# A copy between two places in memory: 8 KB packets cut into 4 KB packets

## The chip, the cores and the metric

The kernel runs on one core of a Trainium2 chip. The core has five engines with instruction queues of their own (TensorE, VectorE, ScalarE called ACT, GpSimd called POOL, and SyncE called SP) and 16 DMA engines that move data. The metric is the device time of one execution in microseconds (us). The time before is the median of three runs, 821.59 us, with runs from 820.93 to 823.31. Lower is better.

## The reference

```python
x = np.random.randn(8192, 8192).astype(np.float32)
return np.fft.ifftshift(x)
```

For even sizes this swaps the quadrants: output row r, column c is input row (r + 4096) mod 8192, column (c + 4096) mod 8192. Nothing is computed, every number only changes its place. The matrix has 8192 x 8192 x 4 bytes = 268.44 MB, and each byte is read once and written once, both in the chip's memory (HBM).

## The kernel before, in words

A row has 32 KB, and each half of it, left or right, is 16 KB that come in one piece from a half row of the input. So the unit of the kernel is the half row.

The kernel consists of DMA copies alone, straight from the input to the output in memory; no tile is loaded into the core. The inner function `copy(queue, row, col, dims)` (line 29 on) makes one copy: it works out the source from the row and column of the output, and issues at line 31 with the access pattern `dims`. Its argument `max_dma_last_dim=piece * 4` bounds the bytes of one contiguous run. `piece` is `hc // 2` = 2048 numbers, so a half row of 4096 numbers (`hc`) becomes two runs of 8192 bytes, and each run is one packet for a DMA engine.

A big copy takes 256 half rows (`rows` = 16 x 16), 4 MB in 512 packets, spread over the 16 DMA engines with 32 packets each, and one more small packet per engine that raises the copy's semaphore when its data has landed. Two queues issue:

- SP issues the left halves (`nc.sync`), 32 copies of 256 half rows.
- ACT issues the right halves (`nc.scalar`), 31 copies of 256 half rows and one of 240. The 16 rows that the last one leaves out go first, in seven small copies of column strips (`strip` = 1024 numbers, runs of 4096 bytes).

The big loop goes through the matrix from the bottom up, in steps of 1024 rows; in each step SP takes the four groups of 256 rows in the order 3, 2, 1, 0, and ACT takes them in the order 1, 0, 3, 2, so that the two queues are two groups apart.

No copy depends on another one's data. The framework gives each copy one of eight semaphores in turn. A copy that gets a semaphore again waits for the copy which had it before, and so each queue has at most four big copies under way at a time. Apart from that, an issuing instruction ends when its packets have found room in the DMA engines' queues. The program ends when SP has seen all eight semaphores at their last value.

Of the kernel before, what the change touches and what calls it, by code (L numbers as in the profile page):

```python
# [1 line left out]

# [4 lines left out]


ENGINES = 16


@with_exitstack
def kernel(
    ctx: ExitStack,
    tc: tile.TileContext,
    x: bass.AP,
    out: bass.AP,
):


    nc = tc.nc
    R, C = x.shape
    hr = R // 2
    hc = C // 2
    per = 16
    rows = ENGINES * per
    piece = hc // 2

    def copy(queue, row, col, dims):
        src = (row + hr) % R * C + (col + hc) % C  # L30
        queue.dma_start(
            out=bass.AP(out.tensor, out.offset + row * C + col, dims),
            in_=bass.AP(x.tensor, x.offset + src, dims),
            max_dma_last_dim=piece * 4,
        )

    start = R - 3 * rows
    strip = hc // 4
    for n, k in enumerate((14, 9, 4)):
        col = hc + n * strip  # L40
        copy(nc.scalar, start + rows - ENGINES, col, [[C, k], [1, strip]])
        copy(nc.scalar, start + rows - ENGINES + k, col, [[C, ENGINES - k], [1, strip]])
    copy(nc.scalar, start + rows - ENGINES, hc + 3 * strip, [[C, ENGINES], [1, strip]])

    for first in range(R - 4 * rows, -1, -4 * rows):
        for n in (3, 2, 1, 0):
            copy(nc.sync, first + n * rows, 0, [[C, rows], [1, hc]])
            right = first + (n + 2) % 4 * rows
            left_out = ENGINES if right == start else 0
            copy(nc.scalar, right, hc, [[C, rows - left_out], [1, hc]])  # L50


# [1 line left out]
_INS = ['x']  # L54
_OUTS = [((8192, 8192), 'float32')]


# [23 lines left out]
```

## Time and profile before

| what | value |
|---|---|
| median of 3 runs | 821.59 us (820.93 to 823.31) |
| the profiled execution | 823.05 us |
| its span, first to last instruction | 821.3 us |
| DMA engines' mean rate | 327 GB/s copied |
| packets | 33888, 268.44 MB |
| share of the span on queue q1 (SP) and q10 (ACT) | 50.6% and 48.4% |
| a big copy, from issue to landing | 102 us |

The profile's page has a strip with a digit for each fortieth of the span, in which 9 stands for DMA engines that are busy for 90% or more, and under it the rate in GB/s. The share of a queue is the time that its packets took, divided by 16 engines times the span. A rate counts each byte once, although it is read and written. The instructions of SP and ACT are listed with the time from their start to their end, which is the time of issuing and not that of moving data. Every copy has the line of `queue.dma_start`, L31, so queues and sizes tell them apart and not lines.

The trace holds a record of each single packet as well: its queue, size, start and duration. It doesn't hold which of the 16 engines ran it.

### The profile page before, as it was taken

To read this page: it belongs to the slowest core of one execution; us is meant where nothing else is said; L and a number is where in the kernel's file an instruction comes from. 1 tells how busy PE (TensorE), PEld (TensorE's weight loads), DVE (VectorE), ACT (ScalarE), POOL (GpSimd) and SP (SyncE) were. 2 spreads that over 40 slices of the span, in tenths; PEclk is the share of its full clock that TensorE was granted. 3 is DMA by queue.
4 is the path that set the end of the run, shared out by engine and by line. 5 is a ranking of instruction groups with operands and counts; after the bars stand their busy time and mean duration, and the time that the engine had idled before them with its cause. 6 is when DMAs were issued, how large, how long until landed. Compare 5 with 4: busy or idle time off the path is not lost. (4 is left out here: it accounts for less than half of the span.)

```text
span 821.3 us, 116 instructions
## 1 busy us (share of the span) xinstructions
POOL 0.2 (0%) x4
## 2 busy tenths in 40 slices
POOL 0000000000000000000000000000000000000000
DMA  9999999999999999999999999999999999999998
GB/s 294 321 328 338 324 329 333 329 331 331 332 329 333 328 330 332 327 328 329 327 334 322 328 322 334 331 327 330 323 331 333 325 332 330 320 330 328 335 326 281
DMA packets 33888, 268.44 MB, mean 327 GB/s; under 512 B 1088, under 2 KB 1088, under 8 KB 1152
## 3 DMA queue, kind: packets, MB, share of 16 engines
q1 hardware_dynamic: 16896, 134.22, 50.6%
q10 hardware_dynamic: 16992, 134.22, 48.4%
HBM read 268.44 MB, written 268.44 MB: 654 GB/s over the span
## 5 line engine op out<-in xcount | busy, mean ns | idle before, releaser
L65 POOL MEMSET const-bfloat16-1.0<- 128x1 bf16 x1 | 0.1, 102 | 0.0
L65 POOL MEMSET const-uint8-127<- 128x1 uint8 x1 | 0.1, 101 | 0.0
L65 POOL MEMSET const-float32-0.0<- 128x1 f32 x1 | 0.1, 99 | 0.2 <-issue 0.2
L65 POOL MEMSET const-float32-1.0<- 128x1 f32 x1 | 0.1, 98 | 0.0
## 6 DMA issues: line engine op xcount, KB each, us to landing
out_dram<-in_x_dram SPq DMA_DIRECT2D x32, 4096.0 KB, 102.0
out_dram<-in_x_dram ACTq DMA_DIRECT2D x31, 4096.0 KB, 102.1
out_dram<-in_x_dram ACTq DMA_DIRECT2D x1, 3840.0 KB, 30.2
out_dram<-in_x_dram ACTq DMA_DIRECT2D x1, 64.0 KB
out_dram<-in_x_dram ACTq DMA_DIRECT2D x1, 56.0 KB
out_dram<-in_x_dram ACTq DMA_DIRECT2D x1, 48.0 KB
out_dram<-in_x_dram ACTq DMA_DIRECT2D x1, 36.0 KB
out_dram<-in_x_dram ACTq DMA_DIRECT2D x1, 28.0 KB
```

What stands on the lines that cost most here:

```text
L65: nc = _bacc.Bacc("TRN2", target_bir_lowering=False, num_devices=1)
```

## The change

`piece` becomes a quarter of a half row instead of a half of it. A half row is then moved as four packets of 4096 bytes one behind the other instead of two of 8192 bytes.

```diff
     per = 16
     rows = ENGINES * per
-    piece = hc // 2
+    piece = hc // 4
 
     def copy(queue, row, col, dims):
         src = (row + hr) % R * C + (col + hc) % C
```

The copies, their order, their queues, their rows and their semaphores stay. The shape of a big copy as the instruction carries it goes from 256x2x2048 to 256x4x1024 numbers, that of the copy of 240 half rows from 240x2x2048 to 240x4x1024. The seven strips have runs of 4096 bytes already and stay as they are.

## The prediction

> **What bounds the kernel now.** I read the page's engine rows first, then the DMA rows, then the queues by stretch, then the issuing instructions.
>
> ```profile
> span 821.3 us, 116 instructions
> ...
> POOL 0.2 (0%) x4
> ...
> DMA  9999999999999999999999999999999999999998
> GB/s 294 321 328 338 324 329 333 329 331 331 332 329 333 328 330 332 327 328 329 327 334 322 328 322 334 331 327 330 323 331 333 325 332 330 320 330 328 335 326 281
> DMA packets 33888, 268.44 MB, mean 327 GB/s; under 512 B 1088, under 2 KB 1088, under 8 KB 1152
> ...
> q1 hardware_dynamic: 16896, 134.22, 50.6%
> q10 hardware_dynamic: 16992, 134.22, 48.4%
> HBM read 268.44 MB, written 268.44 MB: 654 GB/s over the span
> ```
>
> No engine computes; the 16 DMA engines are busy in every slice and the rate is flat. The chain of waits ends after 0.4 us and is of no use here: the end is set by packets alone. Queue q1 carries SP's copies, q10 ACT's. Of the 33888 packets, 1088 are semaphore writes under 512 B, 64 are the 4 KB packets of the seven strips, and the other 32736 are of 8 KB, 2046 for each of 16 engines.
>
> The packets' time: (50.6% + 48.4%) x 16 x 821.3 us = 13010 us. Less 1088 semaphore writes at 9 ns (10 us) and 64 strip packets at 193 ns (12 us), that is 12988 / 32736 = 397 ns for one 8 KB packet. Per engine 2046 x 397 ns = 812 us; the first packet starts at 2.2 us, the last ends at 820.1 us, and the rest is skew between engines and the closing semaphores. The span is therefore packet time, and the question is only what two packets of 4 KB cost against one of 8 KB.
>
> The trace's record of single packets divides the 397 ns: 19535 of the 32736 take 307 to 310 ns, the shortest there are, and the other 13201 take 527 ns in the mean, up to 1476. So an undisturbed 8 KB packet costs 309 ns (424 GB/s over 16 engines), and a mean of 88 ns is stall, spread unevenly: some packets wait long, most not at all.
>
> The strips are the one place where 4 KB packets run, beside 8 KB packets of the other queue. The queue rows of the stretch 5 to 12.4 us, then a stretch's table:
>
> ```profile
> DMA packets 388, 2.53 MB, mean 342 GB/s; under 512 B 50, under 2 KB 50, under 8 KB 108
> ...
> q1 hardware_dynamic: 280, 2.29, 92.5%
> q10 hardware_dynamic: 108, 0.24, 10.1%
> ```
>
> ```profile
> 5.00:12.40 7.40, 0.00 (x0) 1.00 1.03 342
> ...
> 100.00:300.00 200.00, 0.00 (x0) 1.00 1.00 331
> ...
> 804.00:815.00 11.00, 0.00 (x0) 1.00 1.00 333
> ```
>
> Here q1's 280 packets are all of 8 KB, and 0.925 x 16 x 7.4 us / 280 = 391 ns each. Of q10's 108, 50 are semaphore writes and 58 of 4 KB, which take 196 ns in the single record (the rounded share gives 198). Two make 391 ns too: in this stretch a pair costs what one 8 KB packet costs. But it is no ordinary stretch: from 6 to 15 us under a tenth of q1's packets are near 309 ns, where the run has 60%; nearly all are held back a little. In the table the last column is GB/s: one queue alone at the end (333) moves no less than two together (331), so taking turns between queues is not what stalls.
>
> Last come the issuing instructions: those that write the output, SP's waits, and a row of the DMA issues.
>
> ```profile
> L31 ACTq DMA_DIRECT2D out_dram<-in_x_dram x39: 567/20750/27276, 0.7 to 732.1; - x39
> L31 SPq DMA_DIRECT2D out_dram<-in_x_dram x32: 572/18603/22165, 0.7 to 700.7; - x32
> ...
> SPq L31 <- DMA out_dram<-in_x_dram: 240.6, 29, 25.2
> ...
> out_dram<-in_x_dram SPq DMA_DIRECT2D x32, 4096.0 KB, 102.0
> ```
>
> In the first two lines, min, median and max in ns: an issue takes 0.57 us where its queue has room, and some 20 us where it has to wait for room. SP also waits 240.6 us for older copies. Landing 102 us after issue at one copy each 25.5 us per queue means four copies deep.
>
> **The change, part by part.**
>
> *Twice the packets.* Bytes, rows, row order, copies and semaphores stay; 32736 packets become 65472, so 2046 more per engine, all on the path. Their price: the shortest 4 KB packet takes 159 ns, so an undisturbed pair takes 318 against 309, 9 ns more. Ends: if all 9 ns show and the stalls stay, 2046 x 9 = +18.4 us; if stalls shrink by as much, nothing. Below nothing too: all 64 strip packets average 193 ns, a pair 386, which is 11 ns under the run's 397: -22 us. Above: the strip packets that start from 6 to 9 us average 214 ns, a pair 428 against 396 for q1's packets there: +32 ns, +65 us if it held throughout. Between these ends I go by the two rows that compare sizes under one load: packets that are held back anyhow pay nothing (391 against 391), packets at the engine's own pace pay 9 ns (318 against 309), and 60% of the run's packets are of the second kind: 0.6 x 9 = 5.4 ns, 2046 x 5.4 = +11.0 us.
>
> The Trainium skill ("DMA: Bandwidth & Descriptors", section "Why small descriptors are slow") puts the fixed cost at about 3 cycles per packet; at its 850 MHz that is an estimated 3.5 ns, or +7.2 us here in place of the 18.4 us that the shortest packets give, for a median of 829 us. The trace's 9 ns is larger, and the measurement decides; both have the same sign.
>
> *Issue.* All 64 big copies carry twice the packets. A 16-packet strip took 567 ns to issue and a 512-packet copy 572 ns, so packet count costs the issuer nothing while the queue has room. If it doubled, 0.6 us per copy would lie beside the three copies still queued (some 75 us of work): nothing on the path, except about 0.6 us at the very start if that cover is missing.
>
> *Depth.* At the end of a 20.75 us issue about 27 of 33 packets per engine have drained since it began, so 4 x 33 - 27 = 105 packets wait in each engine's queue (an estimate). If that number is the queue's limit, then in 4 KB packets it is 420 KB instead of 840 KB, some 42 us of work per queue. The 16 completions of one copy spread over only 1 to 4 us, so no engine runs dry: nothing. What is late next is the issuer: an issue grows to about 26 us, back to back, and SP's 240.6 us of waits mostly vanish. Nothing else is behind them on SP or ACT. If the queue held under 10 packets this cover would be gone.
>
> *Ends.* The 2.2 us before the first packet and the last microseconds stay.
>
> Sum: the profiled execution took 823.05 us (span 821.3, 1.75 us around it), 1.46 us above the median of 821.59. 823.05 + 11.0 - 1.46 = 832.6, say 833 us.
>
> **The rivals.**
>
> *Memory sets the pace (nothing).* For it: the pair's 391 ns; 327 GB/s in each direction, 654 in all, flat for 800 us, with one queue or two; the engines' own 309 ns would allow 424, and 318 still 412. A slower engine would then merely stall less: 2046 x 0 = 821.6 us. Against it: 60% of packets run at the full 309 ns, so memory is not short at each moment; the packets that start from 12.4 to 35 us move 316 GB/s and those after them 334, so the rate goes with which rows meet, as with conflicts and not a fixed cap. The Trainium skill ("HBM Reference", section "Specifications (TRN2)") gives about 716 GB/s to a domain; 654 is 91% of it, near enough that this rival keeps a chance, not so near as to decide.
>
> *Shorter packets break up the stalls (the other side).* The 527 ns packets hold an engine and the rows it reads and writes; with 4 KB an engine turns to its other queue's rows twice as often, and a blocked stream holds up half as much. It wins once stall falls by over 9 of 88 ns per 8 KB, a tenth. For it: the pair of 386 ns over all strips. Against it: one queue alone, with no other to turn to, is no slower. At 386 ns, 821.6 - 22 = 799 us; at half that gain, 810 us.
>
> *Memory works worse on 4 KB.* Twice as many jumps between streams cause more conflicts, and stall grows. For it: the 428 ns above, and the mean of q1's packets (407 ns from 100 to 700 us) against q10's (386), which shows that row position alone moves 5%. Against it: those are 15 packets. At a third of that price 843 us, at all of it 887.
>
> *The split doesn't happen.* The issued shape changes from 256x2x2048 to 256x4x1024 elements on all 64 copies, so this has next to no chance.
>
> **How the numbers follow.** Less than 0.3% (2.5 us) can't be told from no change here. Part of 9 ns shows, 824 to 840 us: 0.42, predicted 833. Memory paces, 819 to 824: 0.13. Stalls break up, 798 to 819: 0.30. Memory works worse, 840 to 887: 0.15. Faster 0.30, same 0.13, slower 0.57. Cases of both signs count, so the range reaches from 806 (leaving out about a third of the faster case, 0.10) to 850 (leaving out 0.08); the forecast's own range is 824 to 840.
>
> **What would show it.** Queue rows with 66,600 packets, 65,500 of them 4 KB, at 99% share: the split and that packets still set the end. Single packets with a shortest time of 159 ns and a mean near 201 ns ((397 + 5) / 2): the price. A mean of 198 ns says memory paces, 193 that stalls break up, above 206 that memory works worse. ACT and SP issues near 26 us and SP's waits near zero, with landing down to about (105 + 65) x 0.4 = 68 us: the depth. Any stretch with a DMA share under 0.9 would say that queues run dry, and that the depth step is wrong. What would undo the forecast most easily is the stall: at 88 ns of 397 it is ten times the term that I price.

## The result, and the profile after

The changed kernel takes 829.42 us (median of 4 runs, 828.25 to 831.32) against 822.45 us (4 runs, 820.93 to 823.71, three of them those that I had when I predicted). The medians differ by 7.0 us; the ratio is 1.0076, 95% interval 1.0054 to 1.0099, which is 6.3 us (4.4 to 8.1). The forecast was 833 us, 806 to 850. The same kernel was timed again on another chip, where the kernel before is a little faster too: 814.28 us (6 runs) against 811.71 us (20 runs), ratio 1.0041 (1.0027 to 1.0054), which is 3.3 us (2.2 to 4.4). So the sign is firm, and the size differs between the two. From here on they are called the first comparison and the repeat, with their sizes by the ratio.

The profiled execution after took 829.02 us, its span 827.2 us. First the lines of its page that answer to those of before:

```profile
span 827.2 us, 116 instructions
...
DMA  9999999999999999999999999999999999999998
GB/s 293 315 335 329 317 338 327 331 329 324 330 329 329 325 330 324 321 338 326 329 320 325 333 324 322 326 331 326 328 326 318 329 328 324 329 317 323 333 324 274
DMA packets 66624, 268.44 MB, mean 325 GB/s; under 512 B 1088, under 2 KB 1088, under 8 KB 66624
...
q1 hardware_dynamic: 33280, 134.22, 50.1%
q10 hardware_dynamic: 33344, 134.22, 49.6%
```

The packets have doubled, the 1088 semaphore writes have not, and the DMA engines are as full as before. The rate is lower by 2 to 3 GB/s in each of the stretches below, with no gap anywhere. First two stretches of the run before (the last column is GB/s, the one before it the DMA share; it moved 331 from 100 to 300 us and 333 from 804 to 815), then those of the run after:

```profile
300.00:500.00 200.00, 0.00 (x0) 1.00 1.00 329
500.00:700.00 200.00, 0.00 (x0) 1.00 1.00 329
```

```profile
100.00:300.00 200.00, 0.00 (x0) 1.00 1.01 328
300.00:500.00 200.00, 0.00 (x0) 1.00 1.00 327
500.00:700.00 200.00, 0.00 (x0) 1.00 1.00 326
804.00:815.00 11.00, 0.00 (x0) 1.00 1.00 331
```

Then the issuing instructions (min, median and max in ns), SP's waits and a row of the DMA issues, all of the run after:

```profile
L31 ACTq DMA_DIRECT2D out_dram<-in_x_dram x39: 570/25311/28012, 0.7 to 763.3; - x39
L31 SPq DMA_DIRECT2D out_dram<-in_x_dram x32: 654/25169/47445, 0.7 to 724.5; - x32
...
SPq L31 <- DMA out_dram<-in_x_dram: 11.6, 2, 6.6
...
out_dram<-in_x_dram SPq DMA_DIRECT2D x32, 4096.0 KB, 82.1
```

An issue now takes 25 us, one behind the other, and SP's waits for older copies fell from 240.6 to 11.6 us: the issuers wait for room in place of a semaphore. It costs nothing, since the engines never run dry.

One number in these lines does not fit the others. The shares give (50.1% + 49.6%) x 827.2 = 824.7 us of packets per engine, before 99.0% x 821.3 = 813.1: 11.6 us more. But the span grew by only 5.9 us. The records of single packets say what the shares say: a 4 KB packet takes 201.1 ns in the mean (shortest common duration 159), so a pair takes 402.2 against 396.7 ns, and 5.5 ns x 2046 = 11.3 us. Records have grown by twice what the clock shows. The experiments explain that first.

### The profile page after: what moved, and what is told of

The parts are those of the page before. It is cut to its first block, busy times and chain, and to the rows that moved or that the text cites. A ratio compares the mean times of both kernels' runs of the same rounds, so it can differ in the third digit from the quotient of the medians.

```text
span 827.2 us, 116 instructions
## 1 busy us (share of the span) xinstructions
POOL 0.2 (0%) x4
## 2 busy tenths in 40 slices
DMA packets 66624, 268.44 MB, mean 325 GB/s; under 512 B 1088, under 2 KB 1088, under 8 KB 66624
## 3 DMA queue, kind: packets, MB, share of 16 engines
q1 hardware_dynamic: 33280, 134.22, 50.1%
q10 hardware_dynamic: 33344, 134.22, 49.6%
```

## The experiments

### Few engines: what a packet costs an engine with hardly any stall

Only eight copies of 244 half rows are made, in place of the strips and the big loop; the rest of the output is left out. 244 divides by 4 but not by 8, and the rows below show that a quarter of the engines work.

```diff
-    start = R - 3 * rows
...
+    for n in range(4):
+        copy(nc.sync, n * 244, 0, [[C, 244], [1, hc]])
+        copy(nc.scalar, (n + 4) * 244, hc, [[C, 244], [1, hc]])
```

once with `piece = hc // 2`:

> Eight copies of 244 half rows only (the rest of the output is left out); 244 divides by 4 and not by 8, so that I expect 4 engines of the 16 to work, and little stall. 976 packets of 8 KB per engine x 309 ns = 302 us and about 5 us of ends, if packets run back to back without stall. If memory rather than engines set the pace of a packet, more packets would be stalled even so, and the mean stay near 397 ns.

and once with `piece = hc // 4`:

> The same eight copies with 4 KB packets: 1952 x 159 ns = 310 us, 8.8 us more than with 8 KB, if the 9 ns of a pair are the engine's own and lie on the path (the theory). If they are a matter of records that overlap at a packet's end, the span grows by less, down to nothing.

With 8 KB, page rows, and then one stretch:

```profile
span 303.1 us, 53 instructions
...
DMA packets 3936, 31.98 MB, mean 106 GB/s; under 512 B 32, under 2 KB 32, under 8 KB 32
...
q1 hardware_dynamic: 1968, 15.99, 12.5%
q10 hardware_dynamic: 1968, 15.99, 12.4%
```

```profile
20.00:280.00 260.00, 0.00 (x0) 1.00 0.25 107
```

With 4 KB:

```profile
span 307.9 us, 53 instructions
...
DMA packets 7840, 31.98 MB, mean 104 GB/s; under 512 B 32, under 2 KB 32, under 8 KB 7840
...
q10 hardware_dynamic: 3920, 15.99, 12.6%
q1 hardware_dynamic: 3920, 15.99, 12.6%
```

```profile
20.00:280.00 260.00, 0.00 (x0) 1.00 0.26 105
```

Four engines of 16 work, with 976 packets of 8 KB each, and stall has all but gone: the single records have means of 309.8 ns (8 KB) and 159.5 ns (4 KB), with 99.9% at the shortest duration. By the records a pair costs 9.1 ns more than one 8 KB packet. By the clock it costs (307.9 - 303.1) us / 976 = 4.9 ns. The difference is in how records join. In the 8 KB run an engine's packets sum to 976 x 309.8 = 302.4 us, but only 299.4 us pass from the first start to the last end; with 4 KB it is 1952 x 159.5 = 311.3 us in 304.3. So a record reaches some 3 to 4 ns into the next one, and the more packets there are, the more is counted twice. The records' starts and ends show it too: four engines work, but five or six records run at once for 11 us with 8 KB and for 24 us with 4 KB. In the full kernels, more than 16 run at once for 85 us before and for 180 us after. Each variant ran once, so 4.9 ns has no interval.

So the full price of the change on unhindered engines is 2046 x 4.9 = 10.0 us. The 6.3 us of the first comparison are 0.6 of it (0.44 to 0.81), the 3.3 us of the repeat 0.33 of it (0.22 to 0.44).

> The changed kernel itself, against the kernel before on the chip and in the rounds of its neighbours here: the ratio of 1.0076 (1.0054 to 1.0099) again, in a narrower interval. Priced by four lightly loaded engines (4.9 ns per packet added), the whole of the price would be 2046 x 4.9 = 10.0 us, ratio 1.012; 0.6 of it, 1.0073.

This was the repeat, with no edit besides the change itself: 1.0041 (1.0027 to 1.0054). None of the ratios that I had named lies in the interval.

### One size changed: 16 KB and 2 KB

```diff
-    piece = hc // 2
+    piece = hc
```

> A packet's price partly shows on the path (the theory): 1023 packets fewer per engine, each worth the 3.4 us per thousand that the 4 KB kernel paid per packet added (7.0 us for 2046), so about 3.5 us faster than before, ratio 0.996; shortest packet 2 x 309 - 9 = 609 ns. Memory paces: no change, 1.000, since the engine's own pace never mattered. Shorter packets help the stalls (the 4 KB kernel lost less than 9 ns per pair because stalls shrank by turns being shorter): stalls grow with 16 KB and the ratio is at or over 1.00.

819.94 against 821.30 us, ratio 0.9985 (0.9974 to 0.9996). The shortest packets take 608 ns and the commonest 611, where 609 was expected. The gain is small: 1.2 us (0.3 to 2.1) for 1023 packets fewer per engine, 1.2 ns each.

```diff
-    piece = hc // 2
+    piece = hc // 8
```

> The price per packet shows: 6138 more packets per engine than before, at 3.4 ns each +21 us (844 us, ratio 1.026), at 5.4 ns each +33 us (1.040). Memory paces: the engines' own cap would be about 2048 B / 84 ns x 16 = 390 GB/s, still over the 327 that run, so no change, or what 4 KB cost once and no more (1.000 to 1.008). Memory works worse on short runs: more than in proportion, over 1.045.

832.14 against 821.30 us, ratio 1.0128 (1.0092 to 1.0164), 7.6 to 13.5 us. That is far under both prices per packet that I had named; for some 6140 packets more it is 1.7 ns each (1.2 to 2.2). The order 16, 8, 4, 2 KB is the order of the times, so a packet has a price on the path. But the price is well under the 4.9 ns of unhindered engines. The repeat gives 1.6 ns for each packet added (1.1 to 2.1), so one price of some 1.5 ns fits 16, 4 and 2 KB; the first comparison alone, with 3.1 ns (2.2 to 4.0), lies above it. From the page of the run with 2 KB:

```profile
span 833.8 us, 116 instructions
...
DMA packets 132160, 268.44 MB, mean 322 GB/s; under 512 B 1088, under 2 KB 1088, under 8 KB 132160
...
q1 hardware_dynamic: 66048, 134.22, 50.6%
q10 hardware_dynamic: 66112, 134.22, 50.2%
```

The shares add up to over 100%, which shows the double counting again on full load.

### Half of the change

ACT's copies alone, then SP's copies alone, get 4 KB packets:

```diff
-            max_dma_last_dim=piece * 4,
+            max_dma_last_dim=piece * 4 // (2 if queue is nc.scalar else 1),
```

> Only ACT's copies have 4 KB packets, SP's stay at 8 KB. A price per packet: half of the change, +3.5 us, ratio 1.004. A cost of the two queues' mixing, or of one side's rows: the whole of it or none, 1.0076 or 1.000.

821.94 against 821.30 us, ratio 1.0010 (1.0001 to 1.0019): 0.8 us, less than half of the first comparison's 6.3.

```diff
-            max_dma_last_dim=piece * 4,
+            max_dma_last_dim=piece * 4 // (2 if queue is nc.sync else 1),
```

> SP's copies alone with 4 KB packets, ACT's at 8 KB; ACT's alone gave +0.8 us (ratio 1.0001 to 1.0019). A price per packet: the same as that, since the counts are alike. If the left halves were what costs, nearly all of the 7 us.

813.26 against 811.71 us, ratio 1.0018 (1.0007 to 1.0029): 1.5 us. Left and right halves cost alike within their intervals, so the left halves are not what costs. The two halves sum to 2.3 us, which agrees with the 3.3 us of the whole in the repeat (2.2 to 4.4) and not with the 6.3 us of the first comparison (4.4 to 8.1). For each packet added they cost 0.8 ns (0.1 to 1.5) and 1.4 ns (0.6 to 2.3), so the one price of some 1.5 ns fits these two as well. The ACT half was timed on the chip of the 16 KB and 2 KB runs, the SP half on the repeat's.

The run with ACT at 4 KB also did something that I had not foreseen. Its queue rows from 650 to 800 us, and the same stretch as a row of a table:

```profile
DMA packets 12252, 49.40 MB, mean 329 GB/s; under 512 B 192, under 2 KB 192, under 8 KB 12252
...
q10 hardware_dynamic: 12252, 49.40, 100.5%
```

```profile
650.00:800.00 150.00, 0.00 (x0) 1.00 1.01 329
```

SP's packets had all been moved by 609 us, since the queues take turns packet by packet and SP's were twice as large: from 100 to 600 us they moved 109 MB for SP and 55 MB for ACT. From then on ACT's 4 KB packets ran alone, and they moved 329 GB/s: no less than two queues with 8 KB packets did before in that stretch (329), while two queues with 4 KB packets moved 325. That suggested that the turns between two queues, not the packets as such, make 4 KB dear. The run with SP at 4 KB, its mirror image, does not bear this out. There ACT's queue stood empty from 611 to 765 us. Its stretch from 650 to 800 us, in which SP's 4 KB packets have 92% of the packet time, and below it a stretch of the changed kernel with two queues on the same chip:

```profile
650.00:800.00 150.00, 0.00 (x0) 1.00 1.00 332
```

```profile
700.00:800.00 100.00, 0.00 (x0) 1.00 1.00 332
```

One queue of 4 KB packets is no faster here than two.

### No turns: a single queue

All 64 copies go on SP's queue, in turn left and right; the strips go away, and with them the lines for the rows that the strips had taken; the dots stand for those lines.

```diff
...
-            copy(nc.scalar, right, hc, [[C, rows - left_out], [1, hc]])
+            copy(nc.sync, first + (n + 2) % 4 * rows, hc, [[C, rows], [1, hc]])
```

> All 64 copies of 4 MB go on SP's queue, in turn left and right, and no strips: an engine never turns to another queue's rows between packets. If taking turns costs the memory something, faster than before, 0.995 or lower; if not, within 0.3% of it.

> The same single queue with 4 KB packets. If the engine's price per packet is the cause, 6 to 10 us over the single queue with 8 KB, as between the two kernels in question. If turns between two queues' 4 KB packets are the cause (memory works worse on short runs that jump), the same time as the single queue with 8 KB, since its four packets in a row follow one another in memory with nothing in between.

> The single queue with 2 KB packets; with 8 KB and 4 KB it stood at 1.0072 of before. Two queues with 2 KB stood at 1.0128. If the engine's price per packet shows through, four times the packets cost here what they cost on two queues, about 10 us more than the single queue with 8 KB: ratio 1.017 to 1.022. If only turns between queues make short packets dear, no more than with 8 KB: 1.005 to 1.010.

| packets | two queues, ratio to before | one queue, ratio to before |
|---|---|---|
| 8 KB | 1 | 1.0072 (1.0049 to 1.0096) |
| 4 KB | 1.0041 (1.0027 to 1.0054) | 1.0072 (1.0060 to 1.0085) |
| 2 KB | 1.0128 (1.0092 to 1.0164) | 1.0112 (1.0086 to 1.0137) |

The 4 KB row and the single queue's 8 KB row are from one chip; the two 2 KB numbers are from two others, each against the kernel before on its own chip. Both expectations for 8 KB fell: a single queue is slower by 0.7%, so with long packets the turns are not what costs. Stretches of the single queue with 8 KB, early and late, show where it loses:

```profile
5.00:100.00 95.00, 0.00 (x0) 1.00 0.99 324
500.00:700.00 200.00, 0.00 (x0) 1.00 1.00 334
```

From 100 to 300 us it moves 330 GB/s and after that 332 to 334; the changed kernel on the same chip moves 331 to 333 throughout. So in this run the loss lies in the first 300 us, and is not a steady price of having one queue. On one queue the step from 8 to 4 KB then costs 0.0000 with an uncertainty of 0.0027 (the two intervals' half widths combined as a root of squares), that is 0 +- 2.2 us against the 10.0 us of unhindered engines. The step to 2 KB costs 0.0040 +- 0.0035, or 3.3 +- 2.9 us, which lies between the two expectations. So on one queue the price of a 4 KB packet can't be told from nothing, against 3.3 +- 1.1 us on two queues of the same chip; the difference is just clear of the noise. Read by columns, the advantage of two queues shrinks with the packets: 0.7% at 8 KB, 0.3% at 4 KB, none that can be told at 2 KB. Why, no run shows: the single queue also drops the strips and changes which rows meet at a time.

### Packets that do not follow one another

Each copy is cut into column strips of the packet's width, so that an engine's next packet on a queue is in the next row instead of right behind the last.

```diff
-            copy(nc.sync, first + n * rows, 0, [[C, rows], [1, hc]])
+            for col in range(0, hc, piece):
+                copy(nc.sync, first + n * rows, col, [[C, rows], [1, piece]])
```

and the same for ACT's copies, with `piece = hc // 4`:

> 4 KB packets as in the changed kernel, but each copy takes one 4 KB column strip of 256 half rows, so that an engine's next packet on a queue is in the next row, 32 KB on, and not right behind the last. A price per packet alone: as the changed kernel, plus some 3000 more semaphore packets x 9 ns / 16 engines = 1.7 us: about 831 us, ratio 1.010. If memory needs neighbouring packets, so that the four in a row hide part of a cost: clearly slower, over 1.03.

and with `piece = hc // 2`:

> The kernel before with each copy cut into two column strips of 8 KB, so that an engine's next packet on a queue is in the next row. A price per packet alone: as before, plus about 1000 semaphore packets x 9 ns / 16 = 0.6 us, ratio 1.001. Neighbouring packets matter: over 1.01.

With 4 KB 844.20 against 821.30 us, ratio 1.0301 (1.0252 to 1.0349); with 8 KB 826.14 against 822.78 us, ratio 1.0048 (1.0028 to 1.0068). Rows of the run with 4 KB, of its page and of one stretch:

```profile
span 842.1 us, 308 instructions
...
DMA  9999999999999999999999999999999999999997
DMA packets 69698, 268.47 MB, mean 319 GB/s; under 512 B 4160, under 2 KB 4160, under 8 KB 69696
```

```profile
300.00:500.00 200.00, 0.00 (x0) 1.00 1.00 323
```

The DMA engines stay full, and the 3072 additional semaphore writes are 3072 x 9 ns / 16 = 1.7 us. The rest of the 24.7 us, beyond the changed kernel's 3.3 to 6.3, some 17 to 20 us, comes with the new order of the packets. With 8 KB the ratio lies between the two expectations: 3.9 us, of which 0.6 us are semaphore writes. It may be that a 4 KB packet is cheap in the changed kernel because its neighbours in the queue are its neighbours in memory, but that is not shown: these kernels have smaller copies too (1 MB and 2 MB), and which rows the two queues meet at a time shifts; the runs don't separate that from the jumps.

## Why the prediction came out as it did

**What bounds the kernel: right.** Packet time set the span before and after, at a DMA share of 1.00; the issuers' times moved with the change, but beside the path.

**The price of a packet: right in sign, and two terms that were both mis-sized.** The sum was 2046 x 0.6 x 9 ns = 11.0 us; 6.3 us came in the first comparison (4.4 to 8.1), 3.3 in the repeat (2.2 to 4.4). The 9 ns, worked out from the shortest records of both sizes, was the wrong measure: records overlap, and by the clock it is 4.9 ns. The share of 0.6, taken as the part of packets at the engine's own pace, came out as 0.6 in the first comparison, but as 0.33 in the repeat, 0.35 for 2 KB (10.5 us of some 6140 x 4.9 ns = 30 us), and nothing that can be told for 4 KB on one queue. That last case speaks against the rule itself: with 8 KB on one queue 61% of the packets take 307 to 310 ns, as many as in the kernel before, so the rule gives 0.6 x 10.0 = 6 us there, and 0 +- 2.2 came. The first comparison's agreement with 0.6 is luck. The forecast mean of the 4 KB records, 201 ns, was met to 0.1 ns in the first comparison (in the repeat it is 197.9), and the clock still went up by only half of what they say: a record's mean is not the time that a packet takes up.

The strips' stretch said that a pair costs just what one 8 KB packet costs (391 ns each) when nearly all packets are held back. That row was nearer to the truth than the 9 ns, though 7.4 us are too short for a reading of 1%.

**A second source for the price.** The Trainium skill ("DMA: Bandwidth & Descriptors", section "Why small descriptors are slow") gives about 3 cycles per packet, at its 850 MHz an estimated 3.5 ns. I set it aside for the trace's 9 ns. The clock's 4.9 ns on four engines lies between, nearer to that estimate.

**Issue: right.** Twice the packets per copy delayed no engine. **Depth: half right.** Issues of 25 us for 26 forecast and waits of 11.6 us for "near zero" came, and no engine ran dry. But a copy landed after 82 us, not 68: solved for the queue's room, 82 us / 0.402 us - 65 = 139 packets per engine, not 105. The same sum gives some 210 for the run with 2 KB (a landing after 69.8 us), so the runs show no one number of packets as the queue's limit. Nothing in the forecast hung on it.

**The rivals.** "Memory sets the pace" failed as a whole, since 4 KB and 2 KB are slower and 16 KB is faster, but it fits the step from 8 to 4 KB on one queue. "Shorter packets break up the stalls" had at most a part: by the records, what they have over the undisturbed 309 or 159 ns fell from 88 to 2 x (201.1 - 159) = 84 ns per 8 KB; it needed 9. "Memory works worse on 4 KB" as priced, 840 us and more, did not come about with four packets in a row; in the kernel where they do not follow one another, with its smaller copies, the time was 844 us. The split happened.

**What stays open.** Whether the 3 to 6 us that do show are the engines' price or extra stall from the turns between two queues. Half doses on either side, 16 KB, 2 KB and the repeat agree with one price of some 1.5 ns per packet on two queues. The single queue, where 4 KB costs nothing that can be told, speaks for the turns; the stretch of the mirror run, where 4 KB packets alone moved 332 GB/s as two queues do, speaks against them. And why the same pair of kernels differs by 0.41% in one comparison and 0.76% in the other; the two intervals just touch, and chip, runs and chance are not separated.

## What to carry to other kernels

In this copy, whose DMA engines are full and whose 8 KB packets are stalled for 88 of 397 ns, packet length between 16 KB and 4 KB is worth 0.6 to 0.9%; another order of the 4 KB packets, in smaller copies, cost 3%. Price a packet by the clock on a few lightly loaded engines, not by the durations of its records: records overlap, and a share of over 100% is the sign of it. Expect less than that price under full load, and time it more than once, on more than one chip, where the answer is under 1%.

## What was not expected of the hardware

- Records of consecutive packets on one DMA engine overlap by some 3 to 4 ns: 302.4 us of records in 299.4 us, and 311.3 in 304.3.
- Queues take turns by packets and not by bytes: with 8 KB on one and 4 KB on the other, the first was done at 609 us and the second at 819.
- One queue alone was slower than two by 0.72% (0.49 to 0.96) with 8 KB packets, though its DMA share was as high and a stretch of one queue alone within the kernel before had shown no loss (333 GB/s against 331). In its trace the loss lies in the first 300 us.
- Half rows in 16 KB packets beat the kernel before: 0.9985 (0.9974 to 0.9996) of its time. Its issues never wait for room (511 ns each) and SP waits on semaphores instead, to no visible effect.
